# Early phase of a two-layer backbone: written order, other visits, partial sums copied back into PSUM

## The chip, the cores and the metric

The kernel runs on one core of one Trainium2 chip. The metric is the device time of one execution in microseconds (us); three runs of the kernel before took 1402.45, 1407.09 and 1407.42 us, median 1407.09. A difference of about 0.5%, some 7 us, is what a measurement of this kernel can tell from none.

## The reference

There are 256 tokens of width 2048 and two layers. Everything is fp32. Cut to what matters here:

```python
sc = silu(c)                                        # c: one row of 2048
for i in range(2):                                  # layer 0: pooling mixer, layer 1: gMLP
    shift, scale, gate = split(sc @ ada_w[i] + ada_b[i], 3)       # ada_w: 2048 x 6144
    hx = rms_norm(x, norm_g[i]) * (1.0 + scale) + shift           # 256 x 2048
    if i == 0:
        z, g = split(hx @ pool_w_in, 2)                           # 2048 x 8192
        y = (pool_mix(z, w_grp) * pool_scale * silu(g)) @ w_out   # 4096 x 2048
    else:
        u, v, g = gelu / layer_norm / silu parts of hx @ gmlp_w_in   # 2048 x 12288
        y = (u * (w_s @ v + b_s) * silu(g)) @ w_out
    x = x + gate * y
```

The context tokens of the reference do not reach the output here, so the kernel leaves them out.

## The kernel before

**Split products.** A product `a @ w` is done in three fp32r matmuls: `hi·hi`, `hi·lo`, `lo·hi` (L621, L622, L623). For each half of a weight tile ScalarE (ACT) makes `whi` (L98, 128x1024) and VectorE (DVE) `wlo = w - whi` (L99). A *unit* is one 128x512 piece of a weight against 256 tokens: two token halves times three matmuls, six matmuls of 512 columns. There are 960 units, so 5760 such matmuls. A *step* is one half of a weight load: two units. A weight load (`w`, 1 MB) has four units; the buffers `whi` and `wlo` have three places, and step i+2 is split when step i is about to run (`LOOK = 2`).

**The two streams.** Weights (`w`) and the 2048 x 128 pieces of `ada_w` (the `a` loads, 1 MB each) come through one ring of four places (`raw`), in the order of a list that is computed from `CHUNK`, `EARLY` and `LEAD` (L110 to L138). An `a` tile is used by DVE alone: two instructions of 1024 columns, each a product with `sc` and a sum (L245, here called dots). When the last `a` tile of a chunk of the inner dimension (2048 = 16 pieces; chunks of 1, 1, then 2 pieces) has been summed, `start_h` finishes scale and shift (L235 to L238), transposes that part of the normalised x on TensorE (L280), and makes `hh` and `hl`, the split input (L268 to L274).

**The early phase.** Nothing can be multiplied before the first chunk of `hx` is there, and the 32 `a` tiles of layer 0's scale and shift need as much DMA time as 32 weight loads. So the table `EARLY` starts the blocks of `hx @ pool_w_in` with those pieces of the inner dimension that exist: stage s uses only chunks up to s. An entry (b, f, e) is a *visit*: block b, pieces f to e. Block 0 keeps its two PSUM banks through the whole phase (`KEPT`); of the six banks `mm`, the other four (two pairs) serve all other visits in turn. A visit that does not finish its block ends in a copy of its two sums to SBUF by ACT (L637, first visit) or in an add of the sums to that copy by DVE (L628, later visits). Eight stages hold 9, 9, 20, 20, 26, 24, 28 and 16 units, 152 in all.

**Order.** A list scheduler orders the instructions of each engine; `start_h` has high priority. The engines run their lists in order.

Of the kernel before, what the change touches and what calls it, by code (L numbers as in the profile page):

```python
# [13 lines left out]
ALU = mybir.AluOpType  # L14
# [15 lines left out]
LEAD = (0, 1)  # L30
# [35 lines left out]
class Block:  # L66


    def __init__(self, name, nk, lhs, done):
        self.name, self.nk, self.lhs, self.done = name, nk, lhs, done  # L70
        self.ps = self.part = None


@with_exitstack
def backbone(ctx: ExitStack, tc, x, c, ng, adab, ada, w, pscale, band, invcnt, lng, lnb, wsT, bs, out):
# [82 lines left out]
    c_row = st([P, D], F32, "raw", RING)[0:1, :]  # L158
# [18 lines left out]
    nc.scalar.copy(ones_r, ones)  # L177
    for lay in range(2):
        nc.vector.tensor_scalar(ab_sb[:, lay, 1, :], ab_sb[:, lay, 1, :], 1.0, None, op0=ALU.add)
# [3 lines left out]
    bnd = st([P, NG, 2, T], F32R, "cst", 1)  # L183

    def load_late():
        nc.sync.dma_start(out=psc, in_=pscale)
# [8 lines left out]
    sc = sb.tile([P, D], F32, tag="sc", name="sc", bufs=1)  # L195
    for q in range(4):
        ps = bank("mm")
        nc.tensor.matmul(ps, lhsT=ones[0:1, :], rhs=c_row[:, q * CB:(q + 1) * CB], start=True, stop=True)
        nc.scalar.activation(sc[:, q * CB:(q + 1) * CB], ps, AF.Silu)
# [9 lines left out]

    sq0 = const([P, NT, 2], "sq0")  # L210
    for half in range(2):
        for tk in range(NT):
            nc.scalar.activation(big([P, HALF], F32), xin[tk, half], AF.Square, accum_out=sq0[:, tk, half:half + 1])
# [4 lines left out]
    for half in range(2):  # L218
        for tk in range(NT):
            nc.scalar.activation(xin[tk, half], xin[tk, half], AF.Copy, scale=nrm[:, 1, tk:tk + 1])  # L220
# [3 lines left out]
    dots = const([P, 2, 3, KD, 2], "dots")  # L224
# [5 lines left out]
    def vec_of(lay, whats, k0, k1):  # L230

        s = slice(k0, k1)
        for what in whats:
            v = vec[:, lay, what, s]
            nc.vector.tensor_tensor(out=v, in0=dots[:, lay, what, s, 0], in1=dots[:, lay, what, s, 1], op=ALU.add)  # L235
            nc.vector.tensor_tensor(out=v, in0=v, in1=ab_sb[:, lay, what, s], op=ALU.add)
            if what == 1:
                nc.vector.tensor_tensor(out=v, in0=v, in1=ng_sb[:, lay, s], op=ALU.mult)  # L238

    def ada_tile(e, i):  # L240
        lay, what, k = ada_seq[i]
        t = ring_tile[e]
        for half in range(2):
            s = slice(half * HALF, (half + 1) * HALF)
            nc.vector.scalar_tensor_tensor(t[:, s], t[:, s], 1.0, sc[:, s], op0=ALU.mult, op1=ALU.mult,  # L245
                                           accum_out=dots[:, lay, what, k, half:half + 1])
        if (lay or what == 2) and k == KD - 1:
            vec_of(lay, (what,), 0, KD)
        elif lay == 0 and what == 0 and k + 1 in CHUNK:
            with tc.high_priority():  # L250
                start_h(CHUNK.index(k + 1) - 1)
# [4 lines left out]
    def make_h(k0, k1, src, lay, fast=False):  # L256
# [17 lines left out]
        nc.vector.tensor_tensor(out=lo, in0=h[:, s, :], in1=hi.bitcast(F32), op=ALU.subtract)  # L274
# [13 lines left out]

    def start_h(s):
# [15 lines left out]
    def done_z(zb):  # L305
        def go(ps, i):
# [6 lines left out]
            def pool():  # L313
                for half in range(2):
                    qp = bank("aux")
                    for u in range(2):
# [3 lines left out]
                        for z in (zh, zl):  # L320
                            for tk in range(NT):
                                nc.tensor.matmul(o, lhsT=z[:, tk, ct * P:(ct + 1) * P], rhs=bnd[:, g, tk, :], start=(n == 0), stop=(n == 3))  # L322
# [262 lines left out]
    def split_step(i):  # L585

        e = entry_of["w", i // 2]
        if i % 2 == 0:
# [4 lines left out]
        split(src, hi, lo)  # L593
# [4 lines left out]

    nsteps = len(units) // 2
    nsplit = 0  # L600
    for i in range(nsteps):
        while nsplit <= min(i + LOOK, nsteps - 1):
# [4 lines left out]
        for u in range(2):  # L607
            n = 2 * i + u
            blk, k = units[n]
            last = n in breaks or k + 1 == blk.nk  # L610
            if u == 0 or not pair:
# [4 lines left out]
                for tk in range(NT):  # L616
                    for v in ks:
# [3 lines left out]
                        nc.tensor.matmul(blk.ps[tk], lhsT=lh, rhs=rh, start=(new and v == u), stop=False)  # L621
                        nc.tensor.matmul(blk.ps[tk], lhsT=lh, rhs=rl, start=False, stop=False)  # L622
                        nc.tensor.matmul(blk.ps[tk], lhsT=ll, rhs=rh, start=False, stop=end)  # L623
            if last:
                ps, blk.ps = blk.ps, None
                if blk.part is not None:
                    for tk in range(NT):
                        nc.vector.tensor_tensor(out=blk.part[tk], in0=ps[tk], in1=blk.part[tk], op=ALU.add)  # L628
# [91 lines left out]
```

## Time and profile before

| | us |
|---|---|
| median of three runs (lowest, highest) | 1407.09 (1402.45, 1407.42) |
| the profiled execution | 1404.94 |
| its span, first to last instruction | 1403.1 |
| TensorE (PE) busy in the span | 1379.0 (98%) |
| DVE busy | 1010.9 (72%) |
| ACT busy | 672.5 (48%) |
| mean granted TensorE clock | 0.998 |

The span is divided by what the kernel does: no main matmul before 22.35 us, the early phase to about 252 us, the rest after it. PE's busy time counts modelled ends of pipelined matmuls (0.39 us each), though they start 0.226 us apart, so the engine's waits are read from the `[idle before <- releaser]` of its timeline and from how many main matmuls a stretch holds.

### The profile page before, as it was taken

To read this page: it belongs to the slowest core of one execution; us is meant where nothing else is said; L and a number is where in the kernel's file an instruction comes from. 1 tells how busy PE (TensorE), PEld (TensorE's weight loads), DVE (VectorE), ACT (ScalarE), POOL (GpSimd) and SP (SyncE) were. 2 spreads that over 40 slices of the span, in tenths; PEclk is the share of its full clock that TensorE was granted. 3 is DMA by queue.
4 is the path that set the end of the run, shared out by engine and by line. 5 is a ranking of instruction groups with operands and counts; after the bars stand their busy time and mean duration, and the time that the engine had idled before them with its cause. 6 is when DMAs were issued, how large, how long until landed. Compare 5 with 4: busy or idle time off the path is not lost.

```text
span 1403.1 us, 16096 instructions
## 1 busy us (share of the span) xinstructions
PE 1379.0 (98%) x6192; PEld 1136.1 (81%) x6192; DVE 1010.9 (72%) x1305; ACT 672.5 (48%) x792; POOL 0.7 (0%) x6
## 2 busy tenths in 40 slices
PE   6899999999999999999999999999999999999998
PEld 4688887888888888888788888888888888888887
DVE  5899989998998788875765667976665555555553
ACT  8444434554554444444654445545545454544332
POOL 0000000000000000000000000000000000000000
PEclk9999999999999999999999999999999999999999
DMA  8898879878688898896466667776565545556561
GB/s 330 349 337 335 332 295 336 323 300 304 246 325 308 314 352 340 304 347 226 142 264 235 251 222 280 275 257 248 212 243 194 184 180 180 182 186 217 197 214 54
DMA packets 55663, 365.53 MB, mean 261 GB/s; under 512 B 6817, under 2 KB 6817, under 8 KB 13089
## 3 DMA queue, kind: packets, MB, share of 16 engines
q1 hardware_dynamic: 55298, 364.44, 70.2%
q8 instruction: 48, 0.79, 0.2%
q14 instruction: 29, 0.24, 0.0%
q10 hardware_dynamic: 288, 0.07, 0.0%
HBM read 362.38 MB, written 2.10 MB: 260 GB/s over the span
## 4 chain that ended last, share of the span: by engine, by line
PE 91%; DVE 5%; DMA 2%; ACT 1%; issue 1%; SPq 0%; ACTq 0%; DVEq 0%
PE mm L622 29%; PE mm L621 29%; PE mm L623 29%; DVE wlo L99 2%; DVE raw L245 2%; DMA raw<-in_w_dram 1%; PE aux L280 1%; PE aux L322 1%; ACT whi L98 1%; DMA raw<-in_ada_dram 1%; DVE big L628 0%; PE aux L489 0%; PE aux L491 0%; PE aux L490 0%; PE aux L402 0%
## 5 line engine op out<-in xcount | busy, mean ns | idle before, releaser
L99 DVE TENSOR_TENSOR wlo<-raw,whi 128x1024 fp32r<-128x1024 f32 x480 | 585.0, 1223 | 330.3 <-ACT whi L98 328.3
L98 ACT CAST whi<-raw 128x1024 fp32r<-128x1024 f32 x480 | 504.8, 1054 | 655.2 <-PE mm L623 603.1
L621 PE MATMUL mm<-whi,hh 128*128 128x512 f32 x1280 | 497.8, 391 | 4.5 <-ACT whi L98 2.4
L622 PE MATMUL mm<-wlo,hh 128*128 128x512 f32 x1280 | 500.3, 391 | 1.3 <-DVE wlo L99 1.2
L623 PE MATMUL mm<-whi,hl 128*128 128x512 f32 x1280 | 498.7, 390 | 0.0
L621 PEld LDWEIGHTS mm<-whi,hh 128*128 128x128 f32 x1280 | 240.2, 188 | 56.1 <-ACT whi L98 3.9
L622 PEld LDWEIGHTS mm<-wlo,hh 128*128 128x128 f32 x1280 | 240.8, 188 | 53.8 <-DVE wlo L99 4.3
L623 PEld LDWEIGHTS mm<-whi,hl 128*128 128x128 f32 x1280 | 240.7, 188 | 50.1 <-DVE hl L274 0.6
L245 DVE SCALAR_TENSOR_TENSOR raw<-raw,sc 128x1024 f32<-128x1024 f32 x192 | 229.4, 1220 | 17.9 <-DMA raw<-in_ada_dram 17.8
L622 PE MATMUL mm<-wlo,big 128*128 128x512 f32 x512 | 199.3, 389 | 0.0
L623 PE MATMUL mm<-whi,big 128*128 128x512 f32 x512 | 199.2, 389 | 0.0
L621 PE MATMUL mm<-whi,big 128*128 128x512 f32 x512 | 199.2, 389 | 0.0
L622 PEld LDWEIGHTS mm<-wlo,big 128*128 128x128 f32 x512 | 96.1, 188 | 20.3 <-DVE wlo L99 0.4
L623 PEld LDWEIGHTS mm<-whi,big 128*128 128x128 f32 x512 | 96.1, 188 | 19.9
L621 PEld LDWEIGHTS mm<-whi,big 128*128 128x128 f32 x512 | 96.1, 188 | 19.8
L621 PE MATMUL mm<-whi,q 128*128 128x512 f32 x128 | 50.1, 392 | 0.0
L623 PE MATMUL mm<-whi,q 128*128 128x512 f32 x128 | 49.8, 389 | 0.0
L622 PE MATMUL mm<-wlo,q 128*128 128x512 f32 x128 | 49.8, 389 | 0.0
L628 DVE TENSOR_TENSOR big<-mm,big 128x512 f32<-128x512 f32 x52 | 34.0, 684 | 0.4 <-PE mm L623 0.4
L623 PEld LDWEIGHTS mm<-whi,q 128*128 128x128 f32 x128 | 24.0, 188 | 5.0
L622 PEld LDWEIGHTS mm<-wlo,q 128*128 128x128 f32 x128 | 24.0, 188 | 4.9
L621 PEld LDWEIGHTS mm<-whi,q 128*128 128x128 f32 x128 | 24.0, 188 | 4.9
(105 smaller groups left out, 543.7 us busy)
## 6 DMA issues: line engine op xcount, KB each, us to landing
raw<-in_w_dram SPq DMA_DIRECT2D x238, 1024.0 KB, 5.0
raw<-in_ada_dram SPq DMA_DIRECT2D x94, 1024.0 KB, 5.7
big<-in_x_dram SPq DMA_DIRECT2D x4, 512.0 KB, 6.0
raw<-in_ada_dram SPq DMA_DIRECT2D x4, 512.0 KB, 9.0
raw<-in_w_dram SPq DMA_DIRECT2D x4, 512.0 KB, 10.3
q<-in_x_dram SPq DMA_DIRECT2D x8, 256.0 KB, 6.8
gate<-in_lng_dram SPq DMA_DIRECT2D x8, 256.0 KB, 5.0
gate<-in_lnb_dram SPq DMA_DIRECT2D x8, 256.0 KB, 4.3
```

Source lines behind the costliest of these rows:

```text
L98: nc.scalar.copy(hi, src)
L99: nc.vector.tensor_tensor(out=lo, in0=src, in1=hi.bitcast(F32), op=ALU.subtract)
L245: nc.vector.scalar_tensor_tensor(t[:, s], t[:, s], 1.0, sc[:, s], op0=ALU.mult, op1=ALU.mult, accum_out=dots[:, lay, what, k, half:half + 1])
L280: nc.tensor.transpose(tp[:, k - k0, tk * P:(tk + 1) * P], src(k, tk), ident)
L322: nc.tensor.matmul(o, lhsT=z[:, tk, ct * P:(ct + 1) * P], rhs=bnd[:, g, tk, :], start=(n == 0), stop=(n == 3))
L621: nc.tensor.matmul(blk.ps[tk], lhsT=lh, rhs=rh, start=(new and v == u), stop=False)
L622: nc.tensor.matmul(blk.ps[tk], lhsT=lh, rhs=rl, start=False, stop=False)
L623: nc.tensor.matmul(blk.ps[tk], lhsT=ll, rhs=rh, start=False, stop=end)
L628: nc.vector.tensor_tensor(out=blk.part[tk], in0=ps[tk], in1=blk.part[tk], op=ALU.add)
```

## The change

1. PE, DVE and ACT run the early phase in the order in which the code is written (`manual_schedule`), until the first step behind stage 7; then the scheduler takes over.
2. `EARLY` has other visits: 9, 15, 17, 17, 20, 18, 20 and 14 units, 130 in all; fewer and longer returns in the later stages. `LEAD` is (1, 1), so the `a` tiles of stage 0 come one place earlier against the weights.
3. Every visit that does not finish its block copies its sums to SBUF on ACT (62 copies; 26 before). A block that is visited again has its sums copied back into PSUM by ACT (`seed`, 62 copies), when the visit before it begins, and its matmuls add to them. The 74 adds on DVE (L628) are gone.
4. A dot product takes one DVE instruction of 2048 columns, where two of 1024 did it; scale and shift are finished in two small instructions (`vec_of`), where five did it.
5. Of the four sums of squares of x, DVE does two. x is normalised in pieces (128 columns, then 896, the second half at chunk 2), and each chunk's transposes stand one chunk ahead of their use. `hl` is put off behind the next `wlo`. The first `wlo` is made in two pieces. `c` has a place of its own, not one of the ring.

```diff
-LEAD = (0, 1)
+LEAD = (1, 1)
 EARLY = (
     ((0, 0, 1), (1, 0, 1), ... (8, 0, 1)),
-    ((0, 1, 2), (9, 0, 2), (10, 0, 2), (11, 0, 2), (12, 0, 2)),
-    ((0, 2, 4), (1, 1, 4), (2, 1, 4), (3, 1, 4), (4, 1, 4), (5, 1, 4), (6, 1, 4)),
...
-    ((0, 12, 14), (13, 0, 14)),
+    ((0, 1, 2), (9, 0, 2), (10, 0, 2), (11, 0, 2), (12, 0, 2), (13, 0, 2), (14, 0, 2), (15, 0, 2)),
+    ((0, 2, 4), (1, 1, 4), (2, 1, 4), (3, 1, 4), (4, 1, 4), (5, 1, 4)),
...
+    ((0, 12, 14), (15, 2, 14)),
 )
+    ordered = tc.manual_schedule(engines={engine.PE, engine.DVE, engine.Activation})
+    ordered.__enter__()
     for q in range(4):
         ps = bank("mm")
         nc.tensor.matmul(ps, lhsT=ones[0:1, :], rhs=c_row[:, q * CB:(q + 1) * CB], start=True, stop=True)
         nc.scalar.activation(sc[:, q * CB:(q + 1) * CB], ps, AF.Silu)
+        if q < 2:
+            acc = sq0[:, :, q:q + 1]
+            nc.scalar.activation(big([P, HALF], F32), xin[0, q], AF.Square, accum_out=acc[:, 0, :])
+            nc.vector.scalar_tensor_tensor(big([P, HALF], F32), xin[1, q], 1.0, xin[1, q],
+                                           op0=ALU.mult, op1=ALU.mult, accum_out=acc[:, 1, :])
...
-        for half in range(2):
-            s = slice(half * HALF, (half + 1) * HALF)
-            nc.vector.scalar_tensor_tensor(t[:, s], t[:, s], 1.0, sc[:, s], op0=ALU.mult, op1=ALU.mult,
-                                           accum_out=dots[:, lay, what, k, half:half + 1])
+        nc.vector.scalar_tensor_tensor(t, t, 1.0, sc, op0=ALU.mult, op1=ALU.mult, accum_out=dots[:, lay, what, k:k + 1])
+        flush()
...
     def start_h(s):
         k0, k1 = CHUNK[s], CHUNK[s + 1]
-        vec_of(0, (1, 0), k0, k1)
-        tp = transposed(k0, k1, lambda k, tk: xin[tk, k // 8][:, (k % 8) * P:(k % 8 + 1) * P])
-        make_h(k0, k1, tp, 0, fast=(s < 2))
-        if s == 0:
-            warm(8, xin[NT - 1, 0][:, :P])
+        vec_of(0, 0, 2, k0, k1)
+        make_h(k0, k1, xT.pop(s), 0, fast=(s < 2), later=(s > 0))
+        if s == 2:
+            norm_x(HALF, D)
+        if s + 2 < len(CHUNK):
+            transpose_x(s + 1)
+
+    norm_x(0, P)
+    transpose_x(0)
+    warm(9, xin[NT - 1, 0][:, :P])
+    norm_x(P, HALF)
...
+    def seed(j):
+        if j < len(visits) and visits[j].part is not None:
+            blk = visits[j]
+            blk.ps = [bank("mm") for _ in range(NT)]
+            for tk in range(NT):
+                nc.scalar.copy(blk.ps[tk], blk.part[tk])
+            blk.part, blk.seeded = None, True
...
+            if n in visit_at:
+                seed(visit_at[n] + 1)
...
-                if blk.part is not None:
-                    for tk in range(NT):
-                        nc.vector.tensor_tensor(out=blk.part[tk], in0=ps[tk], in1=blk.part[tk], op=ALU.add)
-                    ps = blk.part
-                elif k + 1 < blk.nk:
+                blk.seeded = False
+                if k + 1 < blk.nk:
```

What this does to the lists is seen at two places. On ACT before, around the input of the second and third chunks (`hh_159`, then `h_384` and `hh_382`), with the casts of weights (`whi`) and the copies of ended visits (L637):

```order
L637 COPY big_338<-mm_331 128x512
L268 ACTIVATE hh_159<-aux_305,vec 128x256
L637 COPY big_367<-mm_353 128x512
L637 COPY big_367<-mm_354 128x512
L98 CAST whi_326<-raw_312 128x1024
L98 CAST whi_347<-raw_312 128x1024
L637 COPY big_409<-mm_395 128x512
L637 COPY big_409<-mm_396 128x512
L637 COPY big_432<-mm_418 128x512
L271 ACTIVATE h_384<-aux_377,vec 128x256 x2
L98 CAST whi_391<-raw_320 128x1024
L273 CAST hh_382<-h_384 128x512
```

On ACT now, around the input of the second chunk (`hh_168`), in stage 0:

```order
L99 CAST whi_214<-raw_162 128x1024
L692 COPY q_228<-mm_220 128x512
L692 COPY q_229<-mm_221 128x512
L692 COPY q_240<-mm_232 128x512
L692 COPY q_241<-mm_233 128x512
L278 ACTIVATE hh_168<-aux_174,vec 128x256
L99 CAST whi_257<-raw_185 128x1024
L692 COPY big_270<-mm_262 128x512
L692 COPY big_270<-mm_263 128x512
L692 COPY big_281<-mm_273 128x512
L692 COPY big_281<-mm_274 128x512
L99 CAST whi_284<-raw_185 128x1024
```

Before, the copies of one visit (`big_367`) stand behind `hh_159`, and then two casts; now a cast and the copies of two visits (`big_270`, `big_281`) stand behind `hh_168`, which waits for `vec`.

On ACT now, at the end of stage 1, around the input of the third chunk (`h_414`, `hh_412`); `big_72` and `big_74` are the second half of x, normalised there:

```order
L692 COPY big_380<-mm_366 128x512
L692 COPY big_380<-mm_367 128x512
L99 CAST whi_383<-raw_288 128x1024
L692 COPY big_403<-mm_389 128x512
L692 COPY big_403<-mm_390 128x512
L281 ACTIVATE h_414<-aux_250,vec 128x256 x2
L283 CAST hh_412<-h_414 128x512
L228 ACTIVATE big_72<-big_72,nrm 128x1024
L228 ACTIVATE big_74<-big_74,nrm 128x1024
L99 CAST whi_427<-raw_360 128x1024
L692 COPY big_446<-mm_432 128x512
L692 COPY big_446<-mm_433 128x512
```

Five instructions of the input now stand between the copies of one visit and the next cast, `whi_427`, where before a cast followed the two `h`. On DVE now, at the same place:

```order
L100 TENSOR_TENSOR wlo_363<-raw_288,whi_362 128x1024
L100 TENSOR_TENSOR wlo_384<-raw_288,whi_383 128x1024
L256 SCALAR_TENSOR_TENSOR raw_313,dots<-raw_313,sc 128x2048
L256 SCALAR_TENSOR_TENSOR raw_340,dots<-raw_340,sc 128x2048
L242 TENSOR_TENSOR vec<-dots,ab_sb 128x2x2
L245 TENSOR_TENSOR vec<-vec,ng_sb 128x2
L100 TENSOR_TENSOR wlo_428<-raw_360,whi_427 128x1024
L286 TENSOR_TENSOR hl_413<-h_414,hh_412 128x512
```

The two dots of the chunk stand behind `wlo_384`, which needs `whi_383`, and ahead of `wlo_428`.

## Rows read from the trace of the kernel before

**Rows 1.** The page's part 1: busy us (share of the span), number of instructions.

```profile
PE 1379.0 (98%) x6192; PEld 1136.1 (81%) x6192; DVE 1010.9 (72%) x1305; ACT 672.5 (48%) x792; POOL 0.7 (0%) x6
```

**Rows 2.** Busy time by stretch, L621 alone: stretch, length, PE, PEld (xcount), clock, DMA.

```profile
0.00:22.35 22.35, 0.00 (x0) 0.03 (x1) 1.00 0.90 340
22.35:36.30 13.95, 7.36 (x20) 3.66 (x20) 1.00 0.82 303
36.30:63.45 27.15, 10.53 (x26) 4.92 (x26) 0.94 0.87 350
63.45:252.00 188.55, 103.17 (x270) 50.57 (x270) 1.00 0.89 330
```

**Rows 3.** Busy time by stretch, all: five engines (xcount), clock, DMA share, GB/s.

```profile
45.30:48.50 3.20, 3.20 (x9) 2.42 (x8) 3.20 (x4) 0.31 (x1) 0.00 (x0) 0.50 1.05 425
...
63.45:252.00 188.55, 187.38 (x826) 152.51 (x825) 171.94 (x251) 81.96 (x93) 0.00 (x0) 1.00 0.89 330
...
1250.00:1380.00 130.00, 130.00 (x576) 107.66 (x575) 68.12 (x68) 52.11 (x53) 0.00 (x0) 1.00 0.56 198
```

**Rows 4.** Timeline of PE: start us, us, instruction xcount [idle before <-releaser].

```profile
22.35 1.41 PE L621 MATMUL mm<-whi,hh 128*128 128x512 f32 x5
...
38.45 0.50 PE L621 MATMUL mm<-whi,hh 128*128 128x512 f32 x1 [1.93 <-ACT hh L268]
...
44.02 0.73 PE L621 MATMUL mm<-whi,hh 128*128 128x512 f32 x2 [1.89 <-ACT whi L98]
...
46.24 0.63 PE L623 MATMUL mm<-whi,hl 128*128 128x512 f32 x1
```

**Rows 5.** Groups by form, DVE, 0 to 252 us: busy us, mean ns | idle before.

```profile
L99 DVE TENSOR_TENSOR wlo<-raw,whi 128x1024 fp32r<-128x1024 f32 x80 | 96.7, 1222 | 20.1 <-ACT whi L98 19.6 <-PE mm L622 0.4
...
L245 DVE SCALAR_TENSOR_TENSOR raw<-raw,sc 128x1024 f32<-128x1024 f32 x69 | 82.4, 1220 | 7.2 <-DMA raw<-in_ada_dram 7.2
...
L628 DVE TENSOR_TENSOR big<-mm,big 128x512 f32<-128x512 f32 x32 | 21.0, 685 | 0.4 <-PE mm L623 0.4
...
L274 DVE TENSOR_TENSOR hl<-h,hh 128x512 fp32r<-128x512 f32 x7 | 4.8, 688 | 0.0
...
L269 DVE TENSOR_SCALAR h<-aux,vec 128x256 f32<-128x256 f32 x2 | 1.1, 543 | 2.3 <-ACT hh L268 2.3
L274 DVE TENSOR_TENSOR hl<-h,hh 128x256 fp32r<-128x256 f32 x2 | 0.8, 424 | 0.0
```

**Rows 6.** Groups by form, ACT, 0 to 252 us.

```profile
L98 ACT CAST whi<-raw 128x1024 fp32r<-128x1024 f32 x80 | 83.2, 1055 | 98.8 <-PE mm L623 59.5 <-DMA raw<-in_w_dram 34.4 <-DVE wlo L99 3.1
...
L637 ACT COPY big<-mm 128x512 f32<-128x512 f32 x20 | 11.1, 636 | 9.6 <-PE mm L623 9.6
...
L273 ACT CAST hh<-h 128x512 fp32r<-128x512 f32 x7 | 4.4, 625 | 0.1
...
L220 ACT ACTIVATE big<-big,nrm 128x1024 f32<-128x1024 f32 x4 | 4.4, 1137 | 2.5 <-DVE nrm L207 2.5
```

**Rows 7.** Chain of waits, 30 to 60 us: start us, us, what.

```profile
34.22 2.29 DVE raw L245 x4
...
40.58 0.44 PE aux L280 x4
```

**Rows 8.** Timeline of DVE and ACT: the start, then two places in the phase.

```profile
9.76 0.60 ACT L199 ACTIVATE sc<-mm 128x512 f32<-128x512 f32 x1 [0.49 <-PE mm L198]
...
11.53 1.23 DVE L245 SCALAR_TENSOR_TENSOR raw<-raw,sc 128x1024 f32<-128x1024 f32 x1 [5.42 <-DMA raw<-in_ada_dram]
...
12.44 1.28 ACT L203 ACT_TABLE_LOAD   x1
...
16.46 3.23 ACT L220 ACTIVATE big<-big,nrm 128x1024 f32<-128x1024 f32 x3 [2.53 <-DVE nrm L207]
...
41.94 1.07 ACT L637 COPY big<-mm 128x512 f32<-128x512 f32 x2 [3.54 <-PE mm L623]
...
51.26 1.03 ACT L271 ACTIVATE h<-aux,vec 128x256 f32<-128x256 f32 x2
```

More of the change, by code (lines that the diff above doesn't have):

```diff
@@ L71, in __init__ @@
         self.ps = self.part = None
+        self.seeded = False
 @with_exitstack
@@ L176, in backbone @@
     ones_r = const([P, P], "ones_r", F32R)
-    nc.scalar.copy(ones_r, ones)
-    for lay in range(2):
-        nc.vector.tensor_scalar(ab_sb[:, lay, 1, :], ab_sb[:, lay, 1, :], 1.0, None, op0=ALU.add)
+    nc.vector.tensor_copy(ones_r, ones)
     psc = const([P, KW], "psc")
@@ L192, in load_late @@
             nc.scalar.copy(bnd[:, g], t)
[L195 to L199, printed above, removed]
     def rstd_of(a, r, b):
@@ L207, in rstd_of @@
         nc.vector.scalar_tensor_tensor(r, b, 1.5, r, op0=ALU.add, op1=ALU.mult)
+    sc = sb.tile([P, D], F32, tag="sc", name="sc", bufs=1)
     sq0 = const([P, NT, 2], "sq0")
-    for half in range(2):
-        for tk in range(NT):
-            nc.scalar.activation(big([P, HALF], F32), xin[tk, half], AF.Square, accum_out=sq0[:, tk, half:half + 1])
+    for q in range(4):
+        ps = bank("mm")
+        nc.tensor.matmul(ps, lhsT=ones[0:1, :], rhs=c_row[:, q * CB:(q + 1) * CB], start=True, stop=True)
+        nc.scalar.activation(sc[:, q * CB:(q + 1) * CB], ps, AF.Silu)
+        if q < 2:
[3 more added lines that the diff above has]
+                                           op0=ALU.mult, op1=ALU.mult, accum_out=acc[:, 1, :])
     nrm = const([P, 4, NT], "nrm")
@@ L228, in backbone, with vec_of, flush @@
     ada_seq += [(1, 2, k) for k in range(KD)]
-    def vec_of(lay, whats, k0, k1):
+    def vec_of(lay, w0, w1, k0, k1):
         s = slice(k0, k1)
[L233 to L238, printed above, removed]
+        v = vec[:, lay, w0:w1, s]
+        nc.vector.tensor_tensor(out=v, in0=dots[:, lay, w0:w1, s], in1=ab_sb[:, lay, w0:w1, s], op=ALU.add)
+        if w0 <= 1 < w1:
+            v = vec[:, lay, 1, s]
+            nc.vector.tensor_tensor(out=v, in0=v, in1=ng_sb[:, lay, s], op=ALU.mult)
+    put_off = []
+    def flush():
+        while put_off:
+            put_off.pop(0)()
     def ada_tile(e, i):
@@ L273, in make_h, with low @@
             nc.scalar.copy(hi, h[:, s, :])
-        nc.vector.tensor_tensor(out=lo, in0=h[:, s, :], in1=hi.bitcast(F32), op=ALU.subtract)
+        def low():
+            nc.vector.tensor_tensor(out=lo, in0=h[:, s, :], in1=hi.bitcast(F32), op=ALU.subtract)
+        if later:
+            put_off.append(low)
+        else:
+            low()
     def transposed(k0, k1, src):
@@ L321, in pool @@
                             for tk in range(NT):
-                                nc.tensor.matmul(o, lhsT=z[:, tk, ct * P:(ct + 1) * P], rhs=bnd[:, g, tk, :], start=(n == 0), stop=(n == 3))
+                                nc.tensor.matmul(o, lhsT=z[:, tk, ct * P:(ct + 1) * P], rhs=late["bnd"][:, g, tk, :], start=(n == 0), stop=(n == 3))
                                 n += 1
@@ L587, in split_step @@
         e = entry_of["w", i // 2]
-        if i % 2 == 0:
+        if i % 2 == 0 and i:
             consume_until(e)
@@ L592, in split_step @@
         lo = st([P, 1024], F32R, "wlo", 3)
-        split(src, hi, lo)
+        if i == 0:
+            nc.scalar.copy(hi, src)
+            consume_until(e)
+            for q in range(2):
+                c = slice(q * CB, (q + 1) * CB)
+                nc.vector.tensor_tensor(out=lo[:, c], in0=src[:, c], in1=hi[:, c].bitcast(F32), op=ALU.subtract)
+        else:
+            split(src, hi, lo)
+            flush()
         whl[i] = hi, lo
@@ L597, in split_step @@
             ring_load()
+    visits, visit_at = [], {}
+    for n, (blk, k) in enumerate(units):
+        if not n or units[n - 1][0] is not blk or n - 1 in breaks:
+            visit_at[n] = len(visits)
+            visits.append(blk)
+    def seed(j):
[5 more added lines that the diff above has]
+            blk.part, blk.seeded = None, True
     nsteps = len(units) // 2
@@ L601, in backbone @@
     for i in range(nsteps):
+        if 2 * i >= stage_at[-1] and ordered is not None:
+            ordered.__exit__(None, None, None)
+            ordered = None
         while nsplit <= min(i + LOOK, nsteps - 1):
@@ L610, in backbone @@
             last = n in breaks or k + 1 == blk.nk
+            if put_off and any(units[m][0].nk == KD for m in range(n, n + 2)):
+                flush()
+            if n in visit_at:
+                seed(visit_at[n] + 1)
             if u == 0 or not pair:
```

34 lines of the change are left out of this document (19 added, 15 removed), and 8 rows, old and new, of the table EARLY.

## The prediction

> **What bounds the kernel now.** I read the page's totals first: TensorE (PE) is busy 98% of 1403.1 us [rows 1], so the change can win only what PE loses. Next the count of main matmuls by stretch, which shows where that is. L621 stands twice in each unit. Nothing runs before 22.35 us; then 10 units in 13.95 us; then only 13 units in 27.15 us; then 135 units in 188.55 us [rows 2]. In a full stretch PE starts 576 matmuls in 130 us, one per 0.226 us [rows 3], so a unit costs 6 x 0.226 = 1.36 us. The second stretch should have taken 17.7 us: 9.5 are lost there, less some 0.9 for two groups of transposes. The 135 units need 183.5 us, their six groups of four transposes 6 x 0.44 [rows 7], so about 2.4 of that stretch are lost (1.2 show as idle [rows 3]). All that lies open in the early phase is thus about 11 us, and a few of the 22.35 ahead of it.
>
> The timeline of PE says who was waited for in the bad stretch: 1.93 us for `hh`, 1.89 us for `whi`, after which the clock is granted at 0.50 (1.2 instead of 2.4 GHz) for at least 3.2 us [rows 3, 4]; half of it, 1.6 us, is that price. ACT at the same place stood 3.54 us in front of a copy that waited for PE, with the next casts behind it [rows 8]. DVE is the fullest engine beside PE there (171.94 of 188.55 us [rows 3]). DMA is not the bound: at its fullest it moves 425 GB/s, 2.5 us per load of 1 MB [rows 3].
>
> **What is removed, in capacity.** 74 adds of 0.685 us on DVE [rows 5] are 51 us. They overfilled stage 2: 9.2 of dots, 20 x 0.61 of `wlo`, 8.2 of adds and some 1.5 for the chunk's input are 31 us, against 20 x 1.36 = 27.2 of PE. In stage 1 DVE before had four tiles of 2.29 [rows 7] and 9 x 0.61 of `wlo` [rows 5], 14.7 us, against 9 x 1.36 = 12.2 of PE; now 9.2 + 15 x 0.61 = 18.3 against 20.4. In every stage now DVE's sum is under PE's. One instruction of 2048 columns has no row. Above, it costs the two it replaces, 2.29; below, it costs the 1.22 of one; I take 2.29, since the same elements pass. At the lower end each chunk boundary below would be 1.1 us earlier, 2.1 with two dots in a row. ACT takes 36 more copies of sums and 62 copies back. A copy into PSUM has no row either; the nearest is the copy out of it, 0.636 [rows 6] or 0.54 back to back [rows 8]. I take 0.55, and bound it by 0.3 and 1.06 (half and all of a 1024 cast [rows 6]). Of a stage of 17 units with five visits ACT has 8.9 of casts, 11 of copies both ways and 1.7 of `h`, under PE's 23.1: hidden by capacity. So the sums speak for the change. What decides is the order.
>
> **The start.** Two of four squares leave ACT, so the table load of the root starts after the last Silu (now about 10.85) and not at 12.44 [rows 8]. The root ends at 12.35, four small DVE instructions (some 0.2 each) make it 13.15, two more 13.55. Now the first dot stands behind these: 13.55, where it began at 11.53 [rows 8]. Two dots, 4.6, and `vec`, 0.4, give 18.55; `hh` takes ACT until 19.1. The first matmul starts then, but the second needs `wlo`, and DVE has `h` 0.54, `hl` 0.42 and a 512-column `wlo`, 0.69, in front [rows 5]: 20.8. In effect PE starts at 20.6, against 22.35 [rows 4]: 1.7 us won. The normalising that held `hh` back, 16.46 to 19.7 [rows 8], is hidden under the dots now.
>
> **Stage 0, second chunk.** From 18.55 DVE must do `h` behind `hh`, `hl`, two pieces of `wlo` and one whole, the dot of tile 2, two `wlo`, the dot of tile 3 and `vec`: 0.55 + 0.54 + 0.42 + 1.38 + 1.2 + 2.29 + 2.4 + 2.29 + 0.4 = 11.4, so 29.9. Until then `hh` stands on ACT, and behind it a cast and the copies that would free the one pair of banks that unit 7 needs (block 0 holds a pair for good). `hh` 0.55, cast 1.06, first copy 0.55: 32.1. PE has six units, 20.6 + 8.2 + 0.5 = 29.3: it waits 2.8, and 0.5 more for the next pair.
>
> **Stage 1, third chunk.** The largest wait. From the moment PE ends the first half of the fourth weight load, in a row: drain 0.2 (0.37 shown per matmul [rows 2], less 0.226), that visit's copies 1.1, cast 1.06, `wlo` 1.2, two dots 4.6, `vec` 0.4, `h` 1.03 [rows 8], `hh` 0.63 [rows 6], the second half of x twice 1.06 (within 1.137 [rows 6]), the cast of the sixth load 1.06: 13.4 us. PE holds three halves, 8.2, and transposes 0.4. It is late by 4.8, then 0.6 for the copy that frees the bank and 0.5 for `wlo`: 5.9 us.
>
> **Sum of the first part.** 20.6 + 24 units x 1.36 + 0.9 of transposes + 2.8 + 0.5 + 5.9 = 63.3 us for 24 units; before had 23 at 63.45 [rows 2]. One unit ahead: 1.4 us won. But waits of 2.8 and 5.9 us are longer than the two that came before the half clock; I charge one such drop, 1.6 us. (Two would be 3.2, none 0.)
>
> **Six more chunk boundaries.** At each: drain 0.2, cast 1.06, `wlo` 1.2, dot 2.29, `vec` 0.4, `h` 1.03, `hh` 0.63, cast 1.06, `wlo` 1.2, 9.1 us, against three halves and one matmul, 8.4. Late by about 0.8; at the first of them, where copies and seeds stand between the casts, 1.2: 5.2 in all. Against the 2.4 that the kernel before loses there, 2.8 worse.
>
> **The rest.** Behind 252 us the same matmuls run back to back; the 30 later copies back have ACT half idle around them, and 0 us is put down for them. If that cover were gone, each would be late by at most 1.1 for its pair, which I keep as one such place.
>
> **Result.** -1.4 + 1.6 + 2.8 = +3 us. The profiled execution took 1404.94 us, 1.84 outside its span and 2.15 under the median; +3 gives 1408 against its own time and 1410 against the median. I say 1409: no change that can be told (0.5% is 7 us).
>
> By the Trainium skill, "PSUM — Partial Sum Buffer", section Engine vs sequencer instructions, the queues of ScalarE and VectorE are strictly first in, first out, and matmuls start in program order. That rule speaks against this change: by it nothing passes an `hh` that waits. The 3.54 us of ACT [rows 8] agree.
>
> **Rivals.**
> *Capacity decides (faster).* Then the casts run far enough ahead, and no wait over 0.5 us is left. Won are the 1.7 of the start, 8.6 and 2.4: 12.7 us, 1392 to 1394; with half of it, 1401. For it: DVE's sums now fit in every stage, and DVE was what PE waited for last. Against it: the three places of split weights give three halves, 8.2 us, and the chain of stage 1 is 13.4. Chance 0.22.
> *ACT's seeds stand in front of the cast (slower).* Where visits have three units, copies out (1.1) and back (1.1) come between two casts. If that hits all six boundaries, and not as I have it only the first, five more are late by another 2.2, 11 us, and a half-clock stretch of 1.6 follows at two of them: 3 + 11 + 3.2, some +17, 1422 to 1424. It decides from the point at which a visit ends in the half load ahead of the boundary in most stages. Against it: from stage 4 visits have six to twelve units. Chance 0.18.
> In a sentence by itself: the Trainium skill, "TensorE: Matmul & The Clock Gate", section A second HAM failure mode: psum-queue depth-cycling, tells of short idle spells between groups of matmuls that made the clock swing; by that rule this rival's clock share would come at all six boundaries, 9.6 us instead of 3.2. The trace before has waits under 1 us at full clock and only the one drop [rows 3], so I give it no more.
>
> **How the numbers follow.** Forecast 0.60, faster 0.22, slower 0.18. The forecast's own range, with no or two clock drops (-1.6, +1.6), the dot at its lower end (-7 of the waits at most) and copies at 1.06 (+3): 1401 to 1415. The range for 8 in 10 takes half of the faster case and the near part of the slower: 1398 to 1418. Faster by over 0.5% 0.21, within 0.60, slower 0.19.
>
> **What would show it.** Right: a first matmul near 19 us and the second after a gap; PE idle near 30 us for some 3 and near 52 us for 5 to 6, released by `whi` or a copy; clock 0.5 after one of them; six waits near 1 us on `wlo` or `whi` between 80 and 210 us; no L628-like adds. Wrong: 24 units by 57 us, or DVE done with tile 7 while PE still has work, would make it the faster case; waits of 3 us at most boundaries the slower.

## The result, and the profile after

The changed kernel took 1420.64 us (median of 4 runs, 1417.91 to 1422.42) against 1405.29 us for the kernel before (4 runs): ratio 1.0109, 95% interval 1.0079 to 1.0138. It is 15 us slower; the forecast was 1409, its range ended at 1418. The profiled execution took 1419.12 us with a span of 1417.3, 14.2 us more than that of before. Two versions told of below had one run each far outside the rest (4342.44 and 3600.13 us), and these two are left out of medians and ratios. Three views show where the time went.

The page's part 1, in the columns of [rows 1]:

```profile
PE 1386.2 (98%) x6194; PEld 1140.3 (80%) x6194; DVE 961.8 (68%) x1014; ACT 719.6 (51%) x886; POOL 0.7 (0%) x6
```

DVE has 49 us less to do and ACT 47 more, about what the adds and copies are; PE has two matmuls more and 7 us more of busy time. Since the work of PE is the same but for these two, that is a lower clock (0.993 granted on average, 0.998 before). By stretch, the first of the three main matmuls alone (L679 now, as in [rows 2]: length, PE, PEld, clock, DMA):

```profile
0.00:22.35 22.35, 1.28 (x3) 0.73 (x4) 1.00 0.93 348
22.35:36.30 13.95, 6.25 (x14) 2.98 (x15) 0.88 0.93 357
36.30:63.45 27.15, 12.38 (x28) 5.93 (x29) 0.87 0.79 301
63.45:252.00 188.55, 98.86 (x250) 47.31 (x250) 0.98 0.87 332
```

Up to 63.45 us there are 45 of them, 46 before: no difference, as forecast. Behind that there are 250 where there were 270, 10 units less. Not all of that is loss, for the work that stands between the units at the end of this stretch differs. So here is the start of the same unit in each kernel, unit by unit (a unit is six main matmuls; the start of the first of them, read from the trace):

| unit | before | after | difference |
|---|---|---|---|
| 24 | 65.10 | 65.66 | +0.56 |
| 40 | 87.85 | 87.90 | +0.05 |
| 50 | 101.45 | 110.90 | +9.45 |
| 60 | 116.44 | 125.35 | +8.91 |
| 130 | 212.84 | 224.62 | +11.78 |
| 350 | 537.24 | 549.50 | +12.26 |
| 667 | 985.53 | 999.72 | +14.19 |

The kernel is level with the one before for 88 us, then loses 9.4 us within ten units, 2.3 us up to unit 130, and 2.4 us behind it. The timeline of PE has the four places where it stood longest in the phase (the last is the one at the ten units):

```profile
20.46 0.50 PE L680 MATMUL mm<-wlo,hh 128*128 128x512 f32 x1 [1.14 <-DVE wlo L626]
...
31.30 0.50 PE L679 MATMUL mm<-whi,hh 128*128 128x512 f32 x1 [2.14 <-ACT big L692]
...
57.03 0.79 PE L679 MATMUL mm<-whi,hh 128*128 128x512 f32 x1 [4.25 <-ACT big L692]
...
102.61 0.80 PE L679 MATMUL mm<-whi,hh 128*128 128x512 f32 x1 [6.02 <-ACT whi L99]
```

The first three are the waits of the forecast. The fourth is not in it. (The time in front is the start of the matmul, so each wait ends there.) The timeline of SP's queue, ACT and DVE at that place (start us, us, instruction [idle before <-releaser]), in this order:

```profile
92.83 1.88 SPq L194 DMA_DIRECT2D gs<-in_band_dram  x4
103.84 0.33 SPq L155 DMA_DIRECT2D raw<-in_w_dram  x1
...
91.13 1.12 ACT L647 COPY mm<-big 128x512 f32<-128x512 f32 x2
99.10 2.51 ACT L195 CAST cst<-gs 128x512 fp32r<-128x512 f32 x4 [6.84 <-DMA gs<-in_band_dram]
101.52 1.04 ACT L99 CAST whi<-raw 128x1024 fp32r<-128x1024 f32 x1
...
92.34 1.22 DVE L100 TENSOR_TENSOR wlo<-raw,whi 128x1024 fp32r<-128x1024 f32 x1
102.59 1.23 DVE L100 TENSOR_TENSOR wlo<-raw,whi 128x1024 fp32r<-128x1024 f32 x1 [9.03 <-ACT whi L99]
```

`load_late` issues four loads of the pooling matrix (`in_band`) and casts each of them on ACT (L195), all in one place of the program. In the written order the casts stand right behind their own loads: ACT stands 6.84 us until they land, the cast of the next weight is done at 102.6, and DVE stands 9.03 us in front of the `wlo` that needs it. SP has nothing to issue from 94.7 to 103.8 us, since no place of the ring comes free. In the kernel before, the scheduler had put casts of weights ahead of these four, and ACT ran them without any idle time (the view, from 98 us on, has the last three):

```profile
97.68 1.94 ACT L192 CAST cst<-gs 128x512 fp32r<-128x512 f32 x3
102.75 2.00 ACT L98 CAST whi<-raw 128x1024 fp32r<-128x1024 f32 x2 [3.12 <-DMA raw<-in_w_dram]
```

Around the end of the wait the clock falls to half, as around the end of the earlier ones of 2.14 and 4.25 us (by stretch: five engines (xcount), clock, DMA share, GB/s):

```profile
63.45:252.00 188.55, 181.01 (x803) 147.13 (x802) 145.93 (x145) 118.02 (x167) 0.00 (x0) 0.98 0.87 332
...
100.70:107.50 6.80, 4.43 (x10) 3.18 (x11) 4.91 (x5) 5.38 (x8) 0.00 (x0) 0.50 0.37 126
56.30:63.20 6.90, 6.17 (x14) 4.52 (x15) 4.28 (x4) 4.90 (x9) 0.00 (x0) 0.51 0.36 123
```

By the Trainium skill, "PSUM — Partial Sum Buffer", section Engine vs sequencer instructions, the queue of ScalarE is strictly first in, first out. The 6.84 us agree: nothing passed the casts that waited. (Without them, in the first experiment, the next weight was cast at 95.3 us.)

Durations per instruction, groups by form up to 252 us, DVE and then ACT (busy us, mean ns | idle before):

```profile
L256 DVE SCALAR_TENSOR_TENSOR raw<-raw,sc 128x2048 f32<-128x2048 f32 x36 | 82.1, 2285 | 0.0
...
L692 ACT COPY big<-mm 128x512 f32<-128x512 f32 x48 | 27.0, 590 | 16.5 <-PE mm L681 16.4
L647 ACT COPY mm<-big 128x512 f32<-128x512 f32 x24 | 13.3, 589 | 0.0
...
L281 ACT ACTIVATE h<-aux,vec 128x256 f32<-128x256 f32 x14 | 7.1, 561 | 19.4 <-DVE vec L245 19.4
```

The two prices that no row of before had came out as taken: 2.29 us for the dot, 0.59 for the copy into PSUM (0.55). The last row is one to keep in mind: ACT stands 19.4 us in all in front of `h`, with everything of its list behind it (5.6 us in the kernel before, L271). Whether that costs PE anything is another question; one of the versions below has as much of it and loses little.

### The profile page after: what moved, and what is told of

It reads as the page before. It is cut to its first block, busy times and chain, and to the rows that moved or that the text cites. A ratio compares the mean times of both kernels' runs of the same rounds, so it can differ in the third digit from the quotient of the medians.

```text
span 1417.3 us, 15850 instructions
## 1 busy us (share of the span) xinstructions
PE 1386.2 (98%) x6194; PEld 1140.3 (80%) x6194; DVE 961.8 (68%) x1014; ACT 719.6 (51%) x886; POOL 0.7 (0%) x6
## 4 chain that ended last, share of the span: by engine, by line
PE 83%; DVE 7%; DMA 5%; ACT 3%; issue 2%; SPq 0%; DVEq 0%; ACTq 0%
PE mm L680 27%; PE mm L681 27%; PE mm L679 26%; DVE wlo L100 3%; DVE raw L256 3%; DMA raw<-in_ada_dram 2%; ACT whi L99 1%; PE aux L297 1%; DMA raw<-in_w_dram 1%; PE aux L350 1%; DMA gate<-in_lnb_dram 1%; DMA gate<-in_lng_dram 1%; DMA big<-in_x_dram 0%; DMA gs<-in_band_dram 0%; ACT h L281 0%
## 5 line engine op out<-in xcount | busy, mean ns | idle before, releaser
L679 PE MATMUL mm<-whi,hh 128*128 128x512 f32 x1280 | 503.3, 393 | 13.1 <-ACT whi L99 6.5
L679 PEld LDWEIGHTS mm<-whi,hh 128*128 128x128 f32 x1280 | 241.9, 189 | 65.8 <-ACT whi L99 7.6
L256 DVE SCALAR_TENSOR_TENSOR raw<-raw,sc 128x2048 f32<-128x2048 f32 x96 | 219.4, 2286 | 22.4 <-DMA raw<-in_ada_dram 22.3
L679 PE MATMUL mm<-whi,big 128*128 128x512 f32 x512 | 199.2, 389 | 0.0
L679 PEld LDWEIGHTS mm<-whi,big 128*128 128x128 f32 x512 | 96.1, 188 | 19.9
L679 PE MATMUL mm<-whi,q 128*128 128x512 f32 x128 | 50.1, 392 | 0.0
L692 ACT COPY big<-mm 128x512 f32<-128x512 f32 x48 | 27.0, 590 | 16.5 <-PE mm L681 16.4
L647 ACT COPY mm<-big 128x512 f32<-128x512 f32 x48 | 26.9, 589 | 4.8 <-DVE t L389 4.0
L681 PEld LDWEIGHTS mm<-whi,q 128*128 128x128 f32 x128 | 24.0, 188 | 5.0
```

The costliest lines, as they stand in the source:

```text
L256: nc.vector.scalar_tensor_tensor(t, t, 1.0, sc, op0=ALU.mult, op1=ALU.mult, accum_out=dots[:, lay, what, k:k + 1])
L647: nc.scalar.copy(blk.ps[tk], blk.part[tk])
L692: nc.scalar.copy(blk.part[tk], ps[tk])
```

## Experiments

Differences are given unit by unit as above, so that each loss has a place. They are read from one profiled execution of each version, against that of before. Two of these were the longest of their version: with the band casts later 1420.81 us (median 1415.94), with `h` behind the copies 1408.89 (median 1403.05); both lost 6 to 7 us between units 350 and 667, where the changed kernel lost 1.9. The ends of these two rows are likely worse than a middle run. Each row with "..." is the version with the band casts later and one edit more:

| start of unit, less before's | 24 | 40 | 50 | 60 | 130 | 350 | 667 |
|---|---|---|---|---|---|---|---|
| after | +0.6 | +0.1 | +9.5 | +8.9 | +11.8 | +12.3 | +14.2 |
| band casts later | +0.6 | 0.0 | +0.4 | +6.9 | +10.4 | +9.8 | +15.9 |
| ... and half the `ada` bytes | +0.4 | -0.1 | +0.3 | +0.8 | +4.0 | +3.4 | +4.8 |
| ... and larger visits | -1.7 | -2.2 | -1.7 | -0.7 | +1.0 | +1.4 | +2.3 |
| ... and `h` behind the copies | -8.1 | -8.5 | -2.8 | -3.6 | -0.7 | -2.6 | +4.0 |
| the best version (162 units) | -9.6 | -10.4 | -9.1 | -10.5 | -9.5 | -11.0 | -9.8 |

**The casts of the pooling matrix.** The loads stay where they were, the casts are put off to stage 5:

```diff
         for g in range(NG):
             t = st([P, 2, T], F32, "gs", 4)
             nc.sync.dma_start(out=t, in_=band[g])
-            nc.scalar.copy(bnd[:, g], t)
+            late["raw"].append(t)
...
+    for g in range(NG):
+        after(stage_at[5] + 2 * g + 2, lambda g=g: cast_band(g))
```

> As the changed kernel, but the four casts of the band matrix on ACT stand 37 units behind the issue of their loads, not right behind it. Theory A (in the written order a cast that waits for its own load holds every later cast on ACT): the 6.8 us that ACT stood there, the PE wait of 6.0 us and the half-clock stretch behind it go; the profile has no PE wait over 1 us between 80 and 120 us, and the time falls by 8 to 10 us, to about 1411. Rival B (the 62 copies back into PSUM and the 36 more copies out fill ACT): the casts were only the place where it showed; the wait moves to the next cast, and the time falls by less than 3 us, 1418 or more.

Measured: 1415.94 us (7 runs, 1408.57 to 1420.81, ratio 1.0062, 1.0042 to 1.0082). The wait at 102 us is gone, and unit 50 starts 0.4 us behind before's instead of 9.5. But ten units on 6.5 us are lost again, in a wait of 1.7 us, two under 1 and 6.8 us of half clock, and the time is some 5 us better, not 8 to 10 (the intervals of the two ratios just touch). So the casts cost what the trace says at their place, and a good part of it was hiding another loss. ACT, SP's queue and PE there:

```profile
99.33 0.59 ACT L698 COPY big<-mm 128x512 f32<-128x512 f32 x1 [0.77 <-PE mm L687]
104.32 1.05 ACT L99 CAST whi<-raw 128x1024 fp32r<-128x1024 f32 x1 [4.40 <-DMA raw<-in_w_dram]
...
84.00 0.33 SPq L155 DMA_DIRECT2D raw<-in_ada_dram  x1
90.22 0.33 SPq L155 DMA_DIRECT2D raw<-in_w_dram  x1
...
113.92 0.49 PE L685 MATMUL mm<-whi,hh 128*128 128x512 f32 x1 [1.73 <-ACT whi L99]
```

A weight is late by 4.4 us. Some 15 us earlier SP had nothing to issue from 84.3 to 90.2: the boundary of the chunk held ACT (`h` waits for `vec`), then `wlo`, and no place of the ring came free. DMA didn't make up for it. In the changed kernel PE has no such wait there; that the loads which were out landed while ACT stood at the casts is the likely reason, and was not tested by itself.

**Is it the bytes?** In this one 30 of the 32 `ada` loads of layer 0's scale and shift bring only 1024 columns; the dot takes these twice and writes 16-bit products (2284 ns, as before), so half of each tile is left out of the computation.

```diff
+        if kind == "a" and 2 <= i < 2 * KD:
+            nc.sync.dma_start(out=t[:, :HALF], in_=src[:, :HALF])
+            ring_tile[e] = t
+            return
...
```

> The changed kernel with the band casts put off, and 30 of the 32 ada loads of layer 0's scale and shift halved to 1024 columns (0.5 MB instead of 1); the dot still takes 2048 columns, the same 1024 twice, and the other half of each tile is left out of the computation. Theory DMA: with the band casts out of the way a weight comes 4.4 us late at 104 us since SP had nothing to issue from 84 to 90 us and DMA has no time to make it up; with 38 us less of DMA time the wait and the half clock behind it go: 6 to 8 us under the 1416 of the version with whole loads, 1408 to 1410, while the wait of 4.2 us at 52 us stays. Rival: the chain through ACT and DVE at the boundary sets these waits, not the load: 1413 to 1417.

Measured: 1411.11 us (4 runs, ratio 1.0041, 1.0026 to 1.0056), 5 us less than with whole loads: between the two lines. By stretch, the version with whole loads and then this one:

```profile
104.00:130.00 26.00, 22.50 (x86) 17.43 (x85) 17.19 (x17) 15.81 (x22) 0.00 (x0) 0.87 0.90 334
```

```profile
104.00:130.00 26.00, 25.19 (x112) 20.32 (x111) 19.98 (x19) 16.79 (x25) 0.00 (x0) 1.00 0.70 250
```

112 matmuls instead of 86, and no half clock; unit 60 stands at +0.8 instead of +6.9. The wait at 52 us stayed (4.6 us from one matmul's start to the next), as expected: no load is in that chain. So in the stretch behind 80 us the loads decide, and not the 62 copies each way, which this version has too.

**Is it the number of units for each load?** Stages 2 to 7 with larger visits, 158 units instead of 130, against the same `ada` loads:

```diff
...
-    ((0, 4, 6), (6, 1, 6), (7, 1, 6), (8, 1, 6)),
-    ((0, 6, 8), (9, 2, 8), (10, 2, 8), (11, 2, 8)),
...
+    ((0, 4, 6), (7, 1, 6), (8, 1, 6), (9, 2, 6), (10, 2, 6)),
+    ((0, 6, 8), (11, 2, 8), (12, 2, 8), (13, 2, 8), (1, 4, 8)),
...
```

> The changed kernel with the band casts put off, and from stage 2 on larger visits: stages of 9, 15, 20, 20, 24, 24, 26 and 20 units (158; 9, 15, 17, 17, 20, 18, 20 and 14, 130 in all, in the changed kernel). Each stage still takes the same four ada loads, so the loads have more of PE's time. Theory DMA: what is lost between 80 and 250 us in the version with 130 units (10 us against the kernel before, unit by unit) is the time in which DMA can't make up for the places that came free late; it goes, except for the half of a microsecond at each boundary: 1406 to 1410. The waits of 2.5 and 4.6 us before 57 us stay. Rival: ACT's order at the boundaries sets these waits whatever the loads do: 1413 to 1418.

Measured: 1408.57 us (9 runs, ratio 1.0024, 1.0015 to 1.0034), 7.4 us less than with 130 units, by the table of the visits alone, and inside the line of the loads. Between units 24 and 130 it loses 2.6 us against before, where the 130 units lost 9.9. It has more copies than the version with 130 units, 74 out of PSUM and 74 back instead of 62 and 62, and ACT stands 19.1 us in front of `h` from 66 to 252 us (15.5 there); so neither is what the phase loses by. PE still stood 4.7 us up to 55.4 (from one start to the next).

**The visits of before, in the written order** (`EARLY` and `LEAD` of before, band casts later):

> The changed kernel with the band casts put off (as in the first run of this study) and with the visits and LEAD of the kernel before: 152 units in the early phase, 9 of them in stage 1, and the written order, seeds and dots of 2048 columns kept. Theory order: at each chunk boundary ACT's list stands at the input of the chunk, casts and wlo stop, no place of the weight ring comes free and SP has nothing to issue; that stays with any visits, and stage 1 with 9 units is short of DVE time besides: 1412 to 1420, with waits of 4 to 9 us before 60 us and about 1 us at later boundaries. Rival visits: 130 units instead of 152 against the same 32 ada loads leave DMA too little room, so the old visits take the losses behind 80 us away: 1403 to 1408, and no wait over 0.5 us between 80 and 250 us.

Measured: 1413.08 us (4 runs, ratio 1.0054, 1.0035 to 1.0074). Stage 1 with 9 units costs 2 us (unit 12 at +1.9, unit 24 at +2.1), from there to unit 130 it loses 2.2 us, and some 6 us go in the scheduled part. The time lies at the lower end of the line of the order, with waits of PE of 1.9, 2.4 and 2.7 us before 60 us and none near the 4 to 9 named there. From 80 to 250 us the longest waits are 1.08, 0.77, 0.55 and 0.54 us; that says nearly the same as the last two: with 152 units the loads keep up.

**What stands on ACT at a boundary.** `h`, `hh` and the transposes are put behind the copies of their step, and the second half of x is normalised a stage later:

```diff
+        def rest():
+            make_h(k0, k1, xT.pop(s), 0, fast=(s < 2), later=(s > 0))
+            if s == 3:
+                norm_x(HALF, D)
...
+            held.append((step[0] + (s == 2), rest))
...
+        run_held(i)
```

> As e1_band, and the input of a chunk (h, hh) is made behind the copies of the visits of its step, not ahead of the cast and these copies; the second half of x is normalised one chunk later. Theory A: the other two places where ACT stood ahead of work that was ready, the 2.5 us of PE at 29 us and the 4.6 us at 52 us with 6.8 us of half clock, shrink to 1 to 2 us each; the time falls by 5 to 9 us more, to 1402 to 1406, level with the kernel before or a little faster. Rival B: ACT has the same work, so within 2 us of e1_band. Rival D (the two dots in a row on DVE set the wait at 52 us, not ACT): PE still waits 4 us there, now for wlo.

Measured: 1403.05 us (12 runs, ratio 0.998, 0.9968 to 0.9993), 13 us less than without it, in the line of theory A. Unit 24 starts 8.1 us ahead of before's, at 57.0 us: the waits of 2.1 and 4.2 us and the stretches of half clock at 32 and 56 us are gone (one of 3.4 us stands at 21, another at 86). So these two waits, which the forecast had charged to a chain through dots, were mostly the place of a few instructions on ACT. Not all is kept. From 81 us on the normalising is in the way again, at its new place (ACT, then PE):

```profile
80.10 2.18 ACT L232 ACTIVATE big<-big,nrm 128x1024 f32<-128x1024 f32 x2
82.19 1.98 ACT L99 CAST whi<-raw 128x1024 fp32r<-128x1024 f32 x2
...
85.13 0.50 PE L702 MATMUL mm<-whi,hl 128*128 128x512 f32 x1 [3.79 <-DVE hl L296]
```

With it cut in two instructions that stand two and four steps later:

> The version with h and hh put behind the copies of the step (1403.05 us), and in addition the normalising of the second half of x cut in two instructions that stand two and four steps later. Theory order: the 3.8 us wait of PE for hl at 81 us, and the 3.4 us of half clock behind it, come from 2.18 us of normalising between hh and the next cast; they go, 5 us less: 1397 to 1400. Rival: DVE's wlo and the loads are what is late there, and the wait only moves by a few us: 1402 to 1405.

Measured: 1405.23 us (10 runs, ratio 0.9997, 0.9986 to 1.0008), a miss: no better than the run before. The wait at 81 us only shrank to 2.1 us (2468 ns from one start to the next), with 3.4 us of half clock behind it; ACT there also stood 2.35 us in front of a weight that was loading. That is the rival's line.

**The scheduler instead of the written order**, all else as in the changed kernel (`ordered = None`, `start_h` with high priority):

> As the changed kernel with all its parts, its band casts too, but the list scheduler orders PE, DVE and ACT in the early phase as before, start_h with high priority. Theory A: the written order is what cost the time; the scheduler puts the band casts where their loads have landed, no PE wait over 3 us is left between 45 and 120 us, and the time is 1398 to 1408, level with the kernel before or faster. Rival B or C (the copies on ACT, or the new visits, cost the time): the time stays at 1415 or above.

Measured: 1413.03 us (6 runs, ratio 1.0044, 1.003 to 1.0059): 7.6 us less than in written order, short of what was expected. Nothing is lost at the casts of the pooling matrix (unit 50 at +1.0), the first matmul starts 1.2 us later than before's, and 7.3 us are lost from unit 24 to 130. With 130 units much is lost there in either order (9.9 us in the written one with the band casts later); whether it is the loads here too was not tested.

**Adds on DVE instead of the copies into PSUM**, in written order, band casts later:

```diff
-            if n in visit_at:
-                seed(visit_at[n] + 1)
...
+                if blk.part is not None:
+                    for tk in range(NT):
+                        nc.vector.tensor_tensor(out=blk.part[tk], in0=ps[tk], in1=blk.part[tk], op=ALU.add)
```

> As e1_band, but sums that return are added on DVE as before the change (74 adds of 0.69 us), and none is copied back into PSUM. Rival B: ACT loses 62 copies of 0.59 us, 37 us, so the time falls by 4 us or more against e1_band. Theory A: ACT was not filled, and in the written order an add stands on DVE between two splits and waits for PE; the time stays within 3 us of e1_band or rises by up to 6 us, since DVE then has 1.4 us more per returning visit in stages 2 and 3.

Measured: 1436.68 us (5 runs, ratio 1.0222, 1.0207 to 1.0237), 21 us more than with the copies and outside both lines. The early phase is as slow (unit 130 at +10.6 against +10.4), and 18 us go behind it (unit 350 at +28.7), where PE waits for DVE and three stretches of half clock follow:

```profile
PE aux L354 <- DVE big L100: 10.2, 3, 3.7
```

The phase is as slow without the copies into PSUM. By itself that clears them only in part, since the adds load DVE instead; the runs with half the bytes and with larger visits, which keep the copies and lose little, do the rest. The rival of the prediction that put the loss there has nearly its time (1422 to 1424) but not its mechanism.

**The late dots in halves** (those of layer 0's gate and of layer 1), on the version with the normalising in two pieces:

> As the run with the normalising in two pieces, and the dots behind the early phase (layer 0's gate, all of layer 1) in two instructions of 1024 columns, as before; those of the early phase keep 2048. Theory late dots: the waits of PE for wlo between 450 and 920 us (about 5 us in all, none before) come from dots of 2048 columns that the scheduler puts ahead of wlo; they go: 4 to 6 us less than that run. Rival: DVE stands in front of a load that isn't there yet, whatever the size of the dot: within 2 us of that run.

Measured: 1401.48 us (10 runs, ratio 0.9979, 0.9965 to 0.9992), 3.7 us less than the same with whole dots, between the two lines, and not for the reason expected. The wait at 628 us went (1.5 us idle), and others of 0.4 and 0.3 us came at 328 and 908. Unit by unit the two profiled executions differ ahead of unit 130 (-0.8 and -3.4 us against before), where this edit cuts no dot, and not behind it (-0.7 and -3.5 at unit 667). DVE waits no less for the loads (31.1 us in all, 25.7 with whole dots). They part between units 40 and 50 (-8.1 us at unit 40 in both, then -3.5 and -5.7): there the one with whole dots has 3.4 us of half clock from 85.4 us, behind a wait of PE of 2.07 us, and this one has none behind a wait of 2.04. Half of it, 1.7 us, is most of the 2.2 by which these two executions part there; why the clock fell in one alone, and what made the runs shorter, was not settled.

**Both together.** The version just told, with the larger visits (158 units), and with still larger ones (162):

> The same larger visits (158 units) on the version with h and hh behind the copies, the normalising in two pieces and the late dots of 1024 columns (1401.5 us). Theory DMA: that version is 8.2 us ahead of the kernel before at unit 24 and gives 5 back up to 110 us, where ACT stands 2 to 4 us in front of weights that are still loading; with more units for each load that is kept: 1395 to 1398. Rival: the waits there are the chain through vec, h and the next cast, and stay: 1400 to 1403.

> As the run before, with still larger visits: stages of 9, 15, 23, 23, 24, 26, 24 and 18 units (162). Theory DMA: nothing is lost behind 80 us that wasn't there in the version before, so it is the same time or up to 1.5 us less than that run: 1394 to 1398. Rival: within 1 us of the version with 130 units: 1400 to 1403.

Measured: 1396.54 us (5 runs, ratio 0.9939, 0.9925 to 0.9953) and 1394.49 us (5 runs, ratio 0.9923, 0.9908 to 0.9939), both in the line of the loads. The second is 10.6 us under the kernel before and 26 under the changed one. The early phase by stretch, the version with 130 units and then the one with 162:

```profile
22.35:63.45 41.10, 40.18 (x174) 32.10 (x173) 34.22 (x36) 31.89 (x52) 0.00 (x0) 0.98 0.93 356
63.45:252.00 188.55, 184.71 (x834) 151.89 (x833) 151.99 (x161) 120.81 (x167) 0.00 (x0) 1.00 0.94 348
```

```profile
22.35:63.45 41.10, 40.33 (x179) 32.33 (x178) 35.70 (x36) 32.73 (x53) 0.00 (x0) 1.00 0.98 369
63.45:252.00 188.55, 187.84 (x836) 154.55 (x835) 138.51 (x138) 135.68 (x195) 0.00 (x0) 1.00 0.88 328
```

With 130 units DMA is at 0.94 for 188 us and PE stands 3.8; with 162 it is at 0.88, and PE stands 0.7. What ACT waited for from 66 to 252 us says it too (us in total, times, longest): in the changed kernel, then with 130 units in the mended order, then with 162:

```profile
ACT h L281 <- DVE vec L245: 15.1, 6, 4.1
...
ACT whi L99 <- DMA raw<-in_w_dram: 10.3, 8, 3.2
```

```profile
ACT whi L99 <- DMA raw<-in_w_dram: 27.3, 15, 4.2
```

```profile
ACT whi L99 <- DMA raw<-in_w_dram: 8.2, 6, 2.4
...
ACT h L299 <- DVE vec L253: 1.7, 1, 1.7
```

First ACT stands at `h`; with that gone it stands at weights that are still loading; with more units for each load at neither for long. Such a wait of ACT is not yet a loss: in the kernel before, ACT stood 34.4 us in front of weights in the same stretch ([rows 6] has the same sum up to 252 us) and PE lost 2.4. What PE stood, above, is the measure.

## Why the prediction was wrong

**The start** was right: first matmul at 18.82 (19.1 forecast), second at 20.46 (20.8).

**Stage 0 and stage 1** were right in place and releaser, and somewhat large in size: a wait of 2.14 us from 29.2 (2.8 from 29.3, and 0.5 more, forecast) and one of 4.25 us from 52.8 (5.9 near 52). Unit 24 stood at +0.6 against the kernel before, +0.2 by the sum. That the two agree is luck, for two sizes were off and made up for each other: one drop of the clock was charged with 1.6 us, and there were 3.4 us of half clock at 32.4 and 6.8 at 56.3, a loss of some 4.8 (half of each, without the 0.7 us of the second that lie inside the wait); and without these unit 24 would have started near 60.9 us, not at 63.3, so waits and transposes cost 2.4 less than charged.

**The step that failed: the list of waits.** The sums of the stages held ("In every stage now DVE's sum is under PE's": DVE is busy 145.93 of the 188.55 us from 63.45 on). But "What decides is the order" was then worked out at the chunk boundaries alone; the written order was followed there and nowhere else. `load_late`, whose instructions the diff doesn't touch, stands in that order too: four casts that wait for their own loads, with the phase's casts behind them. The forecast has no term for it. At its place it was 9.4 us of the 14.2, shown by the run in which the casts were moved (unit 50 from +9.5 to +0.4). In the whole time that run won some 5 us, since ten units on a late weight took 6.5 in its place.

**The second half of the step: DMA.** The text set it aside with its fullest rate, 425 GB/s, 2.5 us for a load [rows 3]. The sums of the stages were made for DVE and ACT and not for the loads. At the 348 GB/s that the mended order held for 188 us at a share of 0.94, a load of 1 MB takes 3.0 us; a stage of 17 units has 4.25 + 4 loads, 24.9 us, against 23.1 of PE (an estimate; at a share of 1 the same rate gives 23.4). So a stage with fewer units and the same `ada` loads had no room, and what a boundary took from DMA came back as a late weight. That cost 6.5 us at once in the version without the wait for the casts, and the runs with half the bytes and with larger visits took it away. In the changed kernel itself no such late weight shows at that place: the wait for the casts covers it.

**Six boundaries, 5.2 us, 2.8 more than before:** from unit 50 to 130, where five of them lie, 2.3 us were lost against the kernel before. The matmuls there start late at five places, by 0.3 to 1.0 us, 2.6 in all. Against the kernel before that is about right, by itself half of what was charged, and only the last place is as large as the 0.8 forecast for each. The larger visits suggest that the loads had part in it.

**The rest, 0 us:** 2.4 us from unit 130 to 667. The chain of waits there passes through `ada` loads of layer 1 and the tables of the layer norm, for instance:

```profile
444.53 7.38 DMA raw<-in_ada_dram
...
454.35 7.69 DMA raw<-in_ada_dram
...
890.20 3.10 DMA gate<-in_lnb_dram
```

DVE's list has an instruction that waits for such a load ahead of a `wlo`. No run tested that this is the cause. Why the scheduler puts them so after this early phase and not after that of before was not settled; with the larger visits it costs less than 1.5 us.

**The rivals.** "Capacity decides" stated what the best version does (24 units by 57 us, there by 55.5; 1392 to 1394 forecast, 1394.5 measured), but that version has other visits, another order on ACT and other casts, so the agreement in the number is in part luck; the change as it was written didn't get there. "Seeds in front of the cast" came nearest in time and was wrong: with 74 copies each way instead of 62 the larger visits were faster. "No change", given 0.60, rested on a list of waits that was complete only for the places the diff showed.

## What to carry to other kernels

When a change replaces a scheduler by the written order, read every instruction in that stretch that waits for a load or another engine, those of functions the diff doesn't touch first; each holds back all that is written behind it. Then sum the loads of each stage at the rate that the trace holds over long stretches, as one sums the engines: a stage can have room on every engine and none for its loads, and then a short stop can show as a late weight, here some 15 us on. And a removed wait is to be sought again ten units later before it is booked as won.

## What the runs showed of the hardware

A copy of 128x512 from SBUF into PSUM took ACT 589 ns, one out of PSUM 590. One dot of 2048 columns took DVE 2.29 us, against 2 x 1.22 for two of 1024. Loads ran at 369 GB/s over 41 us in the best version and at 348 over 188 us at a share of 0.94. The Trainium skill, "DMA: Bandwidth & Descriptors", section Where 436 GB/s comes from, gives about 358 GB/s as what binds loads from HBM; the long stretch lies just under that, the 41 us over it, so by this trace the figure did not bind over 41 us. In the early phase the stretches at half clock (0.50 granted, 1.2 GHz) lasted 3.4 or 6.8 us: in the changed kernel 3.4 us behind a wait of PE of 2.14, and 6.8 us each from inside the waits of 4.25 and 6.02; a wait of 2.07 us at 82 us, in the version with the normalising in two pieces, was followed by 3.4 us, and one of 2.04 at the same place, in the version with late dots in halves, by none.
